# Copies of raw weights and squares in PSUM, in two quarters of a feed-forward layer

## The chip, the cores and the metric

The kernel runs on one core of one Trainium2 chip. The metric is the device time of one execution in microseconds; the median of several executions is compared. Before the change it is 1726.33 us (three executions, 1724.89 to 1726.98).

## The reference

One layer of a streaming encoder for 1024 prompt rows and 32 sample rows, 1024 wide: two attention mixers, a gated merge, and a feed-forward part of width 4096. The change lies in the feed-forward part:

```python
h = x + jnp.einsum('bld,de->ble', m, w_out)
u = jnp.einsum('bld,df->blf', rmsnorm(h, g_ffn), w_up)
return h + jnp.einsum('blf,fd->bld', jnp.square(jax.nn.relu(u)), w_down)
```

All of it is in fp32.

## The kernel before

**Products.** An fp32 product is made of three matmuls on operands of the type FP32R: each operand is split into a high part, which ScalarE makes by a cast copy, and a low part, the operand less its high part, which VectorE or GpSimd makes by a subtraction. `three` (one 128-row step) issues wh·xh, wh·xl and wl·xh into one PSUM bank. Weights come in blocks of 128x512 (`raw`, a load on SyncE's queue), `pair` makes the two parts of a block, `parts` those of an activation.

**The feed-forward part.** The rows are worked in groups; the first big group of 512 columns (x is held transposed) goes through `ffn_group`, in four quarters of 1024 hidden units. Quarters 0 and 1 multiply plainly, quarters 2 and 3 in `deep_quarters`. There, each quarter has a step of `ups` for j = 0 to 3 (two blocks of 24 matmuls 128x512 each: u = relu(x·W_up)², in halves of 256 columns) and then `down` for i = 0 to 3. `down` doesn't multiply the four weight blocks w11, w12, w21, w22 of W_down with the four quarters of the activations in eight products, but takes seven (Strassen's way in Winograd's form), of 12 matmuls 128x256 each. For that it needs four sums of weight blocks (s1 = w21 + w22, w21 + w11, w11 + s1, w12 + that) and four sums of activations (T1 to T4), and `gather` adds the products into y. `done` in `ups` makes the activations' parts: in the first block of a step (i = 0) U11 and T1; in the second (i = 1) U21 and U22 (`both`), T3, T2 and T4. The first product of `down` uses U11, the second U21.

**Sums for the second group.** The same weight sums are also written to DRAM (`self.sums`), for w_up too, since a later group reads them there. For w_up the four additions are made by `sums` after a step, and the four stores follow.

**Who sets the order.** Every instruction is recorded by `Plan.record` and issued later by `Plan.run`, engine by engine, in the order of a list scheduler: it takes the ready instruction of the lowest rank (FAST, PREP, MAIN, FILL, SLOW), by times of its own cost model (`cost`), in which VectorE's operations with two inputs in SBUF and GpSimd's lock each other out (`locks`). All instructions have line 412, where `issue` calls them (413 after the change). So an edit in `deep_quarters` can move instructions of the whole stretch. On the chip, each engine works through its queue in that order, and an instruction that waits holds those behind it.

**PSUM.** A core has eight banks of 128x512 fp32: here six with the name `pj` and two with `pd`. In `deep_quarters` `bank()` hands them out in a turn of six pj and two pd. GpSimd can't take part in anything in PSUM in this kernel: whatever it subtracts or adds lies in SBUF.

**Names in the profile.** `ru` are the tiles of relu and square, `xh`/`xl` parts of the last block of activations (`sets`, `third`, `more` hold the sums' parts), `wh`/`wl` parts of weights, `raw`, `wst`, `rb` raw weights, `y` the output sums, `gh`/`gl` the parts of the second group's attention outputs; `xl<-rb`, `xl<-raw` and `xl<-wst` are weight parts kept in the room of x's low part.

Of the kernel before, what the change touches and what calls it, by code (L numbers as in the profile page):

```python
# [47 lines left out]
DEEP = 2  # L48
RAWS, PAIRS, WIDE = 8, 7, 2
ORDER = (*range(8, 16), 5, 6, 7)  # L50
WAIT = (1000, 0, 1500, 0)
# [369 lines left out]
class Layer:  # L421
# [1265 lines left out]
    def ffn_group(self, g, late):  # L1687
# [79 lines left out]
        self.ahead = [row("w_up", 4 * DEEP, i) for i in range(2)]  # L1767
        self.ahead_raws, self.ahead_sums = raws, sums

    def deep_quarters(self, g, qs):  # L1770

        nc, a = self.nc, self.a
        raws, sums = self.ahead_raws, self.ahead_sums
        V, G, add, sub = nc.vector, nc.gpsimd, nc.vector.tensor_add, nc.vector.tensor_sub
# [16 lines left out]
        g.acc = [g.ss[:, cs] for cs in g.chunks]  # L1791
        banks = [lambda: self.bank("pj")[:, :n]] * 6 + [lambda: self.bank("pd")[:, :n]] * 2
        bank = lambda: self.turn("bank", banks)

# [16 lines left out]

        def pair(st, eng):

            with nc.rank(PREP):
                h, l = self.turn("weights", pairs[wide[0]])
                nc.scalar.copy(h, st)
                eng.tensor_sub(l, st, h.bitcast(F32))
            return h, l

        def parts(place, z, eng):  # L1820
            nc.scalar.copy(place[0], z)
            eng.tensor_sub(place[1], z, place[0].bitcast(F32))

        def ups(j, i, units, r0=None):
# [3 lines left out]
            def done(c, cs, ps):  # L1828
                nc.scalar.activation(r, ps, AF.Relu)
                nc.scalar.activation(r, r, AF.Square)  # L1830
                lo, hi = r[:, :n], r[:, n:]
                if i == 0:
                    parts(U11[j], lo, V)
                    sub(lo, lo, hi)
                    parts(T1[j], lo, G)
                    return
                parts(both[j], r, V)
                t, u12 = r0[:, :n], r0[:, n:]
# [9 lines left out]

        def weights(t, engs):

            with nc.rank(PREP):
                w11, w12, w21, w22 = (raw(a["w_down"][i, t]) for i in range(4))
                s1 = raw()

            def keep(i, z):
                with nc.rank(PREP):
                    nc.sync.dma_start(self.sums["w_down", t][i], z)

            def total(out, x, y):
                with nc.rank(PREP):  # L1860
                    add(out, x, y)

            engs = iter(engs)
            yield pair(w11, next(engs))
            yield pair(w12, next(engs))
            total(s1, w21, w22)
            keep(0, s1)
            yield pair(s1, next(engs))
            total(w21, w11, w21)
            keep(2, w21)  # L1870
            total(w11, w11, s1)
            keep(1, w11)
            yield pair(w11, next(engs))
            total(w12, w12, w11)
            keep(3, w12)
            yield pair(w12, next(engs))
            yield pair(w21, next(engs))
            yield pair(w22, next(engs))

# [10 lines left out]
        def down(q, i):  # L1890

            wt = weights(4 * q + i, (V, G, G, G, G, G, G) if q == 3 else (V, G, V, G, G, V, G))

# [33 lines left out]
        for q in qs:  # L1927
            for j in range(4):
                r, st = None, []
                for i in range(2):  # L1930
                    if self.ahead:
                        new, units = self.ahead.pop(0)
                    else:
                        with nc.rank(PREP):
                            new = [raw(a["w_up"][2 * i + k, 4 * q + j]) for k in range(2)]
                        units = [pair(z, G) for z in new]
                    st += new
                    r = ups(j, i, units, r)
                sums("w_up", 4 * q + j, *st)
            if q == 3:  # L1940
# [90 lines left out]
```

## Time and profile before

| what | us |
| --- | --- |
| median of three executions | 1726.33 |
| the profiled execution | 1727.03 |
| its span in the trace | 1725.2 |
| PE busy | 1700.6 |
| VectorE busy | 1273.5 |
| ScalarE busy | 1081.6 |
| GpSimd busy | 1027.0 |
| the stretch of quarters 2 and 3 in the span | 1107 to 1294 |
| PE busy in that stretch | 181.24 of 187 |
| VectorE, ScalarE, GpSimd busy in it | 166.91, 97.57, 148.76 |

About 1.8 us lie outside the span. Times in the views are from the start of the span. In the views a row of a timeline gives start, duration, engine, operation, out<-in, shape and count, and in brackets the time that the engine had been idle and what ended it. The ends of matmuls are modelled, so that consecutive ones overlap, and the distance of their starts is their pace.

### The profile page before, as it was taken

The page shows a single profiled execution, that of the slowest core. Times are in us where ns is not written, and L with a number is a line of the kernel's source. Part 1 is how long each engine was busy: PE and PEld are TensorE (multiplying, and loading weights), DVE is VectorE, ACT ScalarE, POOL GpSimd, SP SyncE. Part 2 cuts the span into 40 slices and gives each one's busy share as a digit, 9 for nine tenths or more (in the row PEclk, how much of TensorE's full clock was granted, in tenths as well). Part 3 has the DMA queues.
Part 4 walks back from the last instruction along what each step waited for, and adds up shares of the span by engine and source line. Part 5 has one row for each costly group of instructions (what it writes and reads, how often), then busy time and mean ns, then how long its engine had stood idle before and what let it go on. Part 6 is the DMA issues. An engine that isn't in the chain of part 4 may idle for free. (4 is left out here: it accounts for less than half of the span.)

```text
span 1725.2 us, 33597 instructions
## 1 busy us (share of the span) xinstructions
PE 1700.6 (99%) x11442; PEld 1577.4 (91%) x11442; DVE 1273.5 (74%) x2599; ACT 1081.6 (63%) x2352; POOL 1027.0 (60%) x850
## 2 busy tenths in 40 slices
PE   8999999999999999999999999999999999999999
PEld 7989999999999989988888888888899999999998
DVE  8567778999556645898986677699975684666577
ACT  6556798873255777777666575554645675747473
POOL 5342333344366675798874454569788794646563
PEclk9999999999999999999999999999999999999999
DMA  7353452444566678556375565546676656555664
GB/s 222 112 168 89 138 170 87 144 142 135 169 183 169 177 205 232 169 153 190 127 234 186 171 199 172 199 173 228 215 258 194 184 168 196 177 173 171 177 185 170
DMA packets 195962, 302.41 MB, mean 175 GB/s; under 512 B 36048, under 2 KB 67376, under 8 KB 195792
## 3 DMA queue, kind: packets, MB, share of 16 engines
q1 hardware_dynamic: 195360, 299.94, 57.0%
q8 instruction: 90, 1.47, 0.4%
q14 instruction: 80, 0.66, 0.1%
q10 hardware_dynamic: 432, 0.34, 0.1%
HBM read 212.39 MB, written 87.70 MB: 174 GB/s over the span
## 5 line engine op out<-in xcount | busy, mean ns | idle before, releaser
L412 PE MATMUL pj<-xh,wh 128*128 128x272 f32 (+2 forms) x1771 | 592.9, 336 | 3.6 <-ACT xh L412 2.9
L412 PE MATMUL pj<-xl,wh 128*128 128x272 f32 (+2 forms) x1771 | 593.9, 336 | 1.2 <-DVE xl L412 1.2
L412 PE MATMUL pj<-xh,wl 128*128 128x272 f32 (+2 forms) x1771 | 593.8, 336 | 0.0
L412 POOL TENSOR_TENSOR wl<-wst,wh 128x512 fp32r<-128x512 f32 x234 | 329.1, 1413 | 206.6 <-ACT wh L412 199.8
L412 PEld LDWEIGHTS pj<-xh,wh 128*128 128x128 f32 x1771 | 333.3, 188 | 33.2 <-ACT xh L412 3.3
L412 PEld LDWEIGHTS pj<-xl,wh 128*128 128x128 f32 x1771 | 333.8, 189 | 29.4 <-DVE xl L412 1.7
L412 PEld LDWEIGHTS pj<-xh,wl 128*128 128x128 f32 x1771 | 333.4, 189 | 27.8
L412 ACT CAST wh<-wst 128x512 fp32r<-128x512 f32 x254 | 156.3, 619 | 108.4 <-PE pj L412 69.5
L412 POOL TENSOR_TENSOR wl<-raw,wh 128x512 fp32r<-128x512 f32 x103 | 157.3, 1535 | 82.8 <-ACT wh L412 65.2
L412 ACT CAST wh<-raw 128x512 fp32r<-128x512 f32 x147 | 90.5, 622 | 81.0 <-PE pj L412 43.2
L412 POOL TENSOR_TENSOR p<-p,rem 128x895 f32<-128x895 f32 (+6 forms) x66 | 106.1, 1621 | 30.5 <-DVE rem L412 26.0
L412 DVE TENSOR_TENSOR tt<-t,tt 128x512 fp32r<-128x512 f32 (+2 forms) x168 | 99.4, 619 | 28.4 <-ACT tt L412 27.4
L412 DVE TENSOR_TENSOR_SCAN rem<-rem 128x896 f32<-128x896 f32 (+6 forms) x66 | 114.9, 1762 | 6.1 <-ACT rem L412 5.8
L412 ACT ACTIVATE junk<-score,cand 128x384 bf16<-128x384 f32 (+1 forms) x124 | 116.0, 936 | 4.3 <-DVE cand L412 2.3
L412 ACT CAST tt<-t 128x512 fp32r<-128x512 f32 (+2 forms) x168 | 84.7, 540 | 45.2 <-PE t L412 33.7
L412 PEld LDWEIGHTS o<-tt,v 128*128 128x128 f32 x640 | 92.6, 188 | 13.2 <-DVE tt L412 2.6
L412 PE MATMUL o<-tt,v 128*128 128x256 f32 (+1 forms) x640 | 99.1, 277 | 3.6 <-DVE tt L412 2.0
L412 PE MATMUL pj<-gh,wh 128*128 128x272 f32 x352 | 101.2, 289 | 0.0
L412 PE MATMUL pj<-gh,wl 128*128 128x272 f32 x352 | 101.1, 289 | 0.0
L412 PE MATMUL pj<-gl,wh 128*128 128x272 f32 x352 | 101.1, 288 | 0.0
L412 PE MATMUL s<-k,q 128*128 128x384 f32 (+5 forms) x384 | 94.0, 354 | 1.4 <-DMA q<-dq 0.8
L412 POOL TENSOR_TENSOR wl<-rb,wh 128x512 fp32r<-128x512 f32 x49 | 70.7, 1443 | 40.6 <-ACT wh L412 34.5
(411 smaller groups left out, 4239.4 us busy)
## 6 DMA issues: line engine op xcount, KB each, us to landing
q<-dq SPq DMA_DIRECT2D x64, 256.0 KB, 5.4
raw<-w_up SPq DMA_DIRECT2D x52, 256.0 KB, 3.2
raw<-w_down SPq DMA_DIRECT2D x52, 256.0 KB, 3.1
k<-dk SPq DMA_DIRECT2D x48, 256.0 KB, 4.0
v<-dv SPq DMA_DIRECT2D x48, 256.0 KB, 4.2
wst<-w_g SPq DMA_DIRECT2D x42, 256.0 KB, 3.4
wst<-w_up SPq DMA_DIRECT2D x37, 256.0 KB, 2.9
wst<-w_down SPq DMA_DIRECT2D x36, 256.0 KB, 3.5
```

Of the source, the lines that this page charges most:

```text
L412: fn(*args, **kw)
```

## The change

In `deep_quarters` alone:

- `copy(z)`: ScalarE copies a raw weight block from SBUF to a `pd` bank. For w_up this is w11 of a step (seven of eight; the first step's blocks are loaded ahead in `ffn_group`), for w_down w11 and w22, 16 copies.
- The low part of a copied block is now made by VectorE, from the copy in PSUM; the low parts of all other blocks by GpSimd. Before, all of w_up were GpSimd's, and of w_down's seven three VectorE's in quarter 2 (one in quarter 3).
- `add_up` makes the four sums, with a copied block read from PSUM where there is one, and each sum's store right behind it; for w_down all four sums stand together after the third pair, and w22's pair is made ahead of them, though used last. Before, the sums stood between the pairs.
- The squares go to the PSUM bank that the block's matmuls filled, and the parts and sums of the activations are read there. For i = 0 the square is now two instructions of 256 columns, since the second half stays in SBUF.
- `bank()` gives the six pj banks in turn; the pd banks are for the copies.

The number of matmuls is the same. The diff:

```diff
--- before.py
+++ after.py
@@ -47,6 +47,7 @@
 SUMS = 3
 DEEP = 2
 RAWS, PAIRS, WIDE = 8, 7, 2
+COPIES = ((0,), (0, 2))
 ORDER = (*range(8, 16), 5, 6, 7)
 WAIT = (1000, 0, 1500, 0)
 TOPK = (("a", [2, 3, 4, 7], (2, 7), 0), ("b", [5, 6, 8], (5, 6), 16))
@@ -1765,12 +1766,12 @@
                             (self.scales if q else self.squares)(g)
                     sums(name, 4 * q + j, *raw)
         self.ahead = [row("w_up", 4 * DEEP, i) for i in range(2)]
-        self.ahead_raws, self.ahead_sums = raws, sums
+        self.ahead_raws = raws
 
     def deep_quarters(self, g, qs):
 
         nc, a = self.nc, self.a
-        raws, sums = self.ahead_raws, self.ahead_sums
+        raws = self.ahead_raws
         V, G, add, sub = nc.vector, nc.gpsimd, nc.vector.tensor_add, nc.vector.tensor_sub
         n = 256
         flat = [z.rearrange("p k t -> p (k t)") for z in (g.mh, g.ml)]
@@ -1789,8 +1790,13 @@
         both = [[z[:, (4 + 2 * k) * n:(6 + 2 * k) * n] for z in flat] for k in range(4)]
         g.chunks = [slice(0, n), slice(n, 2 * n)]
         g.acc = [g.ss[:, cs] for cs in g.chunks]
-        banks = [lambda: self.bank("pj")[:, :n]] * 6 + [lambda: self.bank("pd")[:, :n]] * 2
-        bank = lambda: self.turn("bank", banks)
+        bank = lambda: self.bank("pj")[:, :n]
+
+        def copy(z):
+
+            ps = self.bank("pd")
+            nc.scalar.copy(ps, z)
+            return ps
 
         tmp = nc.open("tmp", "right")
         raws = [raws + [lambda: nc.tile(g.pool, [128, W1], F32, "raw", tag="pb", bufs=3)] * 3,
@@ -1809,12 +1815,15 @@
                 nc.sync.dma_start(z, src)
             return z
 
-        def pair(st, eng):
+        def pair(st, ps=None):
 
             with nc.rank(PREP):
                 h, l = self.turn("weights", pairs[wide[0]])
                 nc.scalar.copy(h, st)
-                eng.tensor_sub(l, st, h.bitcast(F32))
+                if ps is None:
+                    G.tensor_sub(l, st, h.bitcast(F32))
+                else:
+                    sub(l, ps, h.bitcast(F32))
             return h, l
 
         def parts(place, z, eng):
@@ -1827,14 +1836,17 @@
 
             def done(c, cs, ps):
                 nc.scalar.activation(r, ps, AF.Relu)
-                nc.scalar.activation(r, r, AF.Square)
-                lo, hi = r[:, :n], r[:, n:]
                 if i == 0:
+                    lo, t, u12 = ps[:, :n], r[:, :n], r[:, n:]
+                    nc.scalar.activation(lo, t, AF.Square)
+                    nc.scalar.activation(u12, u12, AF.Square)
                     parts(U11[j], lo, V)
-                    sub(lo, lo, hi)
-                    parts(T1[j], lo, G)
+                    sub(t, lo, u12)
+                    parts(T1[j], t, G)
                     return
-                parts(both[j], r, V)
+                nc.scalar.activation(ps, r, AF.Square)
+                lo, hi = ps[:, :n], ps[:, n:]
+                parts(both[j], ps, V)
                 t, u12 = r0[:, :n], r0[:, n:]
                 sub(u12, hi, u12)
                 parts(T3[j], u12, G)
@@ -1846,36 +1858,31 @@
             self.column_block(units, lambda k, cs: (g.h[:, k, cs], g.l[:, k, cs]), done, [slice(0, W1)])
             return r
 
-        def weights(t, engs):
+        def add_up(name, t, w11, w12, w21, w22, s1=None, p11=None, p12=None, p22=None):
+
+            s1 = w22 if s1 is None else s1
+            f = lambda x, y: y if x is None else x
+            for i, out, x, y in ((0, s1, f(p22, w22), w21), (2, w21, f(p11, w11), w21), (1, w11, f(p11, w11), s1),
+                                 (3, w12, f(p12, w12), w11)):
+                add(out, x, y)
+                nc.sync.dma_start(self.sums[name, t][i], out)
+
+        def weights(t):
 
             with nc.rank(PREP):
                 w11, w12, w21, w22 = (raw(a["w_down"][i, t]) for i in range(4))
                 s1 = raw()
-
-            def keep(i, z):
-                with nc.rank(PREP):
-                    nc.sync.dma_start(self.sums["w_down", t][i], z)
-
-            def total(out, x, y):
-                with nc.rank(PREP):
-                    add(out, x, y)
-
-            engs = iter(engs)
-            yield pair(w11, next(engs))
-            yield pair(w12, next(engs))
-            total(s1, w21, w22)
-            keep(0, s1)
-            yield pair(s1, next(engs))
-            total(w21, w11, w21)
-            keep(2, w21)
-            total(w11, w11, s1)
-            keep(1, w11)
-            yield pair(w11, next(engs))
-            total(w12, w12, w11)
-            keep(3, w12)
-            yield pair(w12, next(engs))
-            yield pair(w21, next(engs))
-            yield pair(w22, next(engs))
+                p11, p12, p22 = (copy(z) if i in COPIES[1] else None for i, z in enumerate((w11, w12, w22)))
+            yield pair(w11, p11)
+            yield pair(w12, p12)
+            x22 = pair(w22, p22)
+            with nc.rank(PREP):
+                add_up("w_down", t, w11, w12, w21, w22, s1, p11, p12, p22)
+            yield pair(s1)
+            yield pair(w11)
+            yield pair(w12)
+            yield pair(w21)
+            yield x22
 
         def product(wt, xs, ps=None):
             first = ps is None
@@ -1889,7 +1896,7 @@
 
         def down(q, i):
 
-            wt = weights(4 * q + i, (V, G, G, G, G, G, G) if q == 3 else (V, G, V, G, G, V, G))
+            wt = weights(4 * q + i)
 
             def gather(e, c, ps, sign, when):
                 cs = g.chunks[c]
@@ -1926,17 +1933,22 @@
 
         for q in qs:
             for j in range(4):
-                r, st = None, []
+                r, st, ps = None, [], {}
                 for i in range(2):
                     if self.ahead:
                         new, units = self.ahead.pop(0)
                     else:
                         with nc.rank(PREP):
                             new = [raw(a["w_up"][2 * i + k, 4 * q + j]) for k in range(2)]
-                        units = [pair(z, G) for z in new]
+                            if i == 0 and 0 in COPIES[0]:
+                                ps["p11"] = copy(new[0])
+                            if i and 2 in COPIES[0]:
+                                ps["p22"] = copy(new[1])
+                        got = [ps.get("p11"), None] if i == 0 else [None, ps.get("p22")]
+                        units = [pair(z, p) for z, p in zip(new, got)]
                     st += new
                     r = ups(j, i, units, r)
-                sums("w_up", 4 * q + j, *st)
+                add_up("w_up", 4 * q + j, *st, **ps)
             if q == 3:
                 self.reload(g, 2)
             for i in range(4):
```

How the queues change, at the end of quarter 3's up blocks. ScalarE before; the last block's relu and square are the two rows ACTIVATE ru_14467, U21 and U22 get their high parts by CAST xh1_222<-ru_14467 128x512, and wh are high parts of weights:

```order
L412 CAST xl0_221<-rb_224 128x512 [waits DMAHW5_49,PE_49]
L412 CAST wh_14501<-raw_14494 128x512 [waits DVE_49]
L412 ACTIVATE ru_14467<-pj_14468 128x512 [waits PE_49,Activation_49]
L412 ACTIVATE ru_14467<-ru_14467 128x512 [waits Activation_49]
L412 CAST wh_14504<-raw_14490 128x512 [waits DVE_49]
L412 CAST xh1_222<-ru_14467 128x512 [waits Activation_49]
L412 CAST wh_14506<-raw_14491 128x512 [waits DVE_49]
```

ScalarE after at the same place (the last block's square now goes to its bank, pj_14483):

```order
L413 CAST wh_14525<-raw_14507 128x512 [waits PE_49]
L413 ACTIVATE ru_14482<-pj_14483 128x512 [waits PE_49,Pool_49]
L413 ACTIVATE pj_14483<-ru_14482 128x512 [waits Activation_49]
L413 CAST wh_14527<-raw_14508 128x512 [waits PE_49]
L413 CAST xh1_222<-pj_14483 128x512 [waits DVE_49]
L413 CAST sets_14265<-ru_14474 128x256
L413 CAST sets_14265<-ru_14474 128x256 [waits DVE_49]
L413 CAST xh1_222<-pj_14483 128x256 [waits DVE_49]
```

In both a weight cast stands between the square and the cast of U21 and U22: before it waits for a sum of VectorE's, now for PE, which frees its room. The cast of U21 and U22 now waits for VectorE, which reads the same bank ahead of it.

VectorE before, at the same place; the four rows raw are the weight sums of a w_down step, and ru_14459<-ru_14467,ru_14459 is the first difference of the last block (u12):

```order
L412 TENSOR_TENSOR ru_14459<-ru_14459 128x256 [waits DVE_49]
L412 TENSOR_TENSOR raw_14494<-raw_14492,raw_14493 128x512 [waits DMAHW4_49,DMAHW3_49,DMAHW1_49]
L412 TENSOR_TENSOR raw_14492<-raw_14490,raw_14492 128x512 [waits DVE_49]
L412 TENSOR_TENSOR raw_14490<-raw_14490,raw_14494 128x512 [waits DMAHW2_49,DVE_49]
L412 TENSOR_TENSOR raw_14491<-raw_14491,raw_14490 128x512 [waits DMAHW0_49,DVE_49,Pool_49]
L412 TENSOR_TENSOR ru_14459<-ru_14467,ru_14459 128x256 [waits Activation_49]
L412 TENSOR_TENSOR xl1_223<-ru_14467,xh1_222 128x512 [waits Activation_49]
L412 SCALAR_TENSOR_TENSOR ru_14459<-ru_14459,ru_14467 128x256 [waits Pool_49]
L412 TENSOR_TENSOR y0_6599<-pj_14474,y0_6599 128x256 [waits PE_49]
L412 SCALAR_TENSOR_TENSOR ru_14467<-ru_14459,ru_14467 128x256 [waits DVE_49]
```

VectorE after:

```order
L413 TENSOR_TENSOR ru_14474<-pj_14475,ru_14474 128x256 [waits Activation_49]
L413 TENSOR_TENSOR xl1_223<-pj_14475,xh1_222 128x256
L413 TENSOR_TENSOR xl0_221<-pd_14535,xl0_221 128x512 [waits PE_49,Activation_49]
L413 TENSOR_TENSOR y0_6599<-pj_14491,y0_6599 128x256 [waits PE_49]
L413 TENSOR_TENSOR ru_14474<-pj_14483,ru_14474 128x256 [waits DVE_49,Activation_49]
L413 SCALAR_TENSOR_TENSOR ru_14474<-ru_14474,pj_14483 128x256 [waits Activation_49,Pool_49]
L413 TENSOR_TENSOR xl1_223<-pj_14483,xh1_222 128x512
L413 SCALAR_TENSOR_TENSOR pj_14483<-ru_14474,pj_14483 128x256 [waits DVE_49]
L413 TENSOR_TENSOR sets_14265<-ru_14474,sets_14265 128x256 [waits Activation_49]
```

The four sums no longer stand ahead of the difference; the y row, a gather, does, and an operation on the bank pj_14483 waits for ScalarE's casts of it.

ScalarE before, at the end of quarter 2's up blocks (the last block's rows are ru_14319):

```order
L412 CAST third_14267<-ru_14303 128x256 [waits DVE_49]
L412 CAST xh1_222<-ru_14311 128x256 [waits DVE_49]
L412 ACTIVATE ru_14319<-pj_14320 128x512 [waits PE_49,Activation_49,Pool_49]
L412 ACTIVATE ru_14319<-ru_14319 128x512 [waits Activation_49]
L412 CAST xh1_222<-ru_14319 128x512 [waits Activation_49]
```

ScalarE after there; the two COPY rows are the copies of w11 and w22 of the first w_down step:

```order
L413 COPY pd_14375<-raw_14370 128x512 [waits DMAHW5_49,DVE_49]
L413 CAST xh1_222<-ru_14314 128x256 [waits DVE_49]
L413 COPY pd_14376<-raw_14373 128x512 [waits DMAHW0_49,DVE_49]
L413 CAST wh_14364<-raw_14348 128x512 [waits PE_49]
L413 ACTIVATE ru_14322<-pj_14323 128x512 [waits PE_49]
L413 ACTIVATE pj_14323<-ru_14322 128x512 [waits Activation_49]
L413 CAST wh_14366<-rb_224 128x512 [waits DVE_49,PE_49]
L413 CAST xh1_222<-pj_14323 128x512 [waits DVE_49]
```

The copies, which wait for a load each (DMAHW) and for VectorE, stand ahead of the last block's relu, and one weight cast too; the cast of the bank pj_14323 waits for VectorE.

## The prediction

> **What bounds the kernel now.** I read the page's first part, then the table of windows over the last two quarters of the first group, then PE's waits there, and then the timelines of ScalarE (ACT), VectorE (DVE) and GpSimd (POOL) ahead of the two largest waits.
>
> ```profile
> PE 1700.6 (99%) x11442; PEld 1577.4 (91%) x11442; DVE 1273.5 (74%) x2599; ACT 1081.6 (63%) x2352; POOL 1027.0 (60%) x850
> ```
>
> TensorE bounds the program: it is busy in 1700.6 of 1725.2 us. The change leaves the number of matmuls as it is, so it can only win back time in which PE stands still or runs below its pace, and only in the stretch that it touches. The table of windows shows that stretch (us; busy time and instructions of PE, PEld, DVE, ACT, POOL; granted clock; DMA share; GB/s):
>
> ```profile
> 1150.00:1162.00 12.00, 9.78 (x77) 9.13 (x76) 10.85 (x21) 4.97 (x10) 4.82 (x4) 1.00 0.66 224
> 1162.00:1182.00 20.00, 19.95 (x167) 19.62 (x166) 19.82 (x30) 9.25 (x16) 14.56 (x10) 1.00 0.73 250
> 1182.00:1200.00 18.00, 16.93 (x118) 15.26 (x119) 14.15 (x18) 7.48 (x13) 17.35 (x12) 1.00 0.60 191
> 1242.00:1252.00 10.00, 7.89 (x53) 7.39 (x52) 9.88 (x11) 6.33 (x13) 10.00 (x8) 0.83 1.05 407
> 1262.00:1282.00 20.00, 20.00 (x170) 20.00 (x169) 16.63 (x37) 11.51 (x19) 16.59 (x13) 1.00 0.87 282
> 1282.00:1294.00 12.00, 11.69 (x92) 11.25 (x92) 5.40 (x13) 5.43 (x9) 11.56 (x9) 1.00 0.90 290
> ```
>
> 1262 to 1282 is a clean stretch of w_down products: 20.00 / 170 = 0.1176 us for one 128x256 matmul. By that pace the 77 matmuls of 1150 to 1162 need 9.06 us, so 2.94 are lost there; the 53 of 1242 to 1252 need 6.23, so 3.77 are lost. In the other two windows wider matmuls are mixed in, so I take only what isn't busy: 1.07 (18.00 - 16.93) and 0.31 (12.00 - 11.69). With 0.05 from 1162 to 1182 the stage loses **8.1 us**. Since a modelled end hides part of each gap, the true loss may be some 1 us more; I carry 9.2 as the ceiling. PE's waits (engine, what it waited for: us in total, times, longest), first for 1149 to 1200, then for 1240 to 1294, name who is late:
>
> ```profile
> PE pj L412 <- DVE xl L412: 1.2, 1, 1.2
> PE pj L412 <- ACT xh L412: 0.8, 1, 0.8
> PE pd L412 <- DVE y L412: 0.8, 1, 0.8
> PE pd L412 <- POOL wl L412: 0.3, 1, 0.3
> PE pj L412 <- DVE y L412: 0.2, 1, 0.2
> ```
>
> ```profile
> PE pj L412 <- ACT xh L412: 2.1, 1, 2.1
> PE pj L412 <- DVE pj L412: 0.3, 1, 0.3
> ```
>
> Both large losses stand where a quarter's up blocks end and its w_down products begin: PE needs the parts of the last block's activations, and these are late. The timelines around the second such boundary show why, PE first, then ACT, then DVE (start, us, operation, in brackets the idle time before it and what ended it):
>
> ```profile
> 1239.65 0.40 PE L412 MATMUL pj<-xh,wl 128*128 128x512 f32 x1
> ...
> 1243.15 0.28 PE L412 MATMUL pd<-xl,wh 128*128 128x256 f32 x1
> 1245.49 0.38 PE L412 MATMUL pj<-xh,wh 128*128 128x256 f32 x1 [2.06 <-ACT xh L412]
> ...
> 1247.15 0.41 PE L412 MATMUL pj<-xl,wh 128*128 128x256 f32 x1
> ```
>
> ```profile
> 1241.11 0.62 ACT L412 CAST xl<-rb 128x512 fp32r<-128x512 f32 x1
> 1241.63 0.62 ACT L412 CAST wh<-raw 128x512 fp32r<-128x512 f32 x1
> 1242.15 0.59 ACT L412 ACTIVATE ru<-pj 128x512 f32<-128x512 f32 x1
> 1242.77 0.63 ACT L412 ACTIVATE ru<-ru 128x512 f32<-128x512 f32 x1
> 1244.30 0.62 ACT L412 CAST wh<-raw 128x512 fp32r<-128x512 f32 x1 [0.90 <-DVE raw L412]
> 1244.82 0.61 ACT L412 CAST xh<-ru 128x512 fp32r<-128x512 f32 x1
> ```
>
> ```profile
> 1240.68 5.25 DVE L412 TENSOR_TENSOR raw<-raw 128x512 f32<-128x512 f32 x4
> 1245.86 1.51 DVE L412 TENSOR_TENSOR ru<-ru 128x256 f32<-128x256 f32 x1
> ```
>
> The last up matmul starts at 1239.65, and PE has other products until 1243.3. But the square is done only at 1243.4, and the cast xh<-ru that PE waits for stands on ACT behind a weight cast that waits for DVE's sums. Those four sums take 5.25 us, 1.3 each. After the wait of 2.06 us PE falls to the pitch of half a clock (0.41 in place of 0.28 for one modelled matmul); this is the 0.83 in the windows' clock column, and makes the other 1.7 us of the 3.77.
>
> At the first boundary the chain is of the same kind (POOL, DVE, ACT and PE):
>
> ```profile
> 1138.09 5.78 POOL L412 TENSOR_TENSOR wl<-raw,wh 128x512 fp32r<-128x512 f32 x1 [3.11 <-issue]
> ```
>
> ```profile
> 1144.60 1.50 DVE L412 SCALAR_TENSOR_TENSOR ru<-ru 128x256 f32<-128x256 f32 x1 [1.91 <-POOL xl L412]
> ```
>
> ```profile
> 1151.76 0.41 ACT L412 CAST xh<-ru 128x256 fp32r<-128x256 f32 x1 [2.08 <-DVE ru L412]
> 1152.07 0.59 ACT L412 ACTIVATE ru<-pj 128x512 f32<-128x512 f32 x1
> ```
>
> ```profile
> 1149.93 0.39 PE L412 MATMUL pj<-xh,wl 128*128 128x512 f32 x1
> ...
> 1154.03 0.50 PE L412 MATMUL pj<-xh,wh 128*128 128x256 f32 x2 [0.83 <-ACT xh L412]
> ```
>
> DVE and POOL hold each other up: POOL's subtraction took 5.78 us, DVE then waited for POOL, and the relu of the last block began at 1152.07, 1.7 us after that block's last matmul had ended (1149.93 + 0.39). PE would have gone on at 1153.2 (1154.03 less its 0.83). How far the two stretch each other, the groups of this stage say (count: minimum/median/maximum ns):
>
> ```profile
> L412 DVE TENSOR_TENSOR y<-pj,y x23: 405/412/692, 1100.3 to 1279.9; 128x256 f32<-128x256 f32 x21, 128x512 f32<-128x512 f32 x2
> L412 DVE TENSOR_TENSOR raw<-raw x32: 677/1220/1821, 1133.2 to 1271.6; 128x512 f32<-128x512 f32 x32
> L412 DVE TENSOR_TENSOR wl<-raw,wh x10: 677/1286/1796, 1138.0 to 1232.5; 128x512 fp32r<-128x512 f32 x10
> ```
>
> ```profile
> L412 POOL TENSOR_TENSOR wl<-raw,wh x43: 1297/1711/5775, 1106.1 to 1264.5; 128x512 fp32r<-128x512 f32 x43
> ```
>
> An operation of DVE with an input in PSUM never took over 0.69 us. One with both inputs in SBUF takes between 0.68 and 1.8, and POOL's go up to 5.8.
>
> **The change, part by part.** *Copies.* ScalarE makes 7 copies of w_up blocks and 16 of w_down blocks, 128x512 each. No ScalarE write to PSUM stands in this trace; the nearest rows are
>
> ```profile
> L412 ACT CAST wh<-raw 128x512 fp32r<-128x512 f32 x53 | 32.0, 619 | 30.5 <-DVE raw L412 14.1 <-PE pj L412 10.4 <-PE pd L412 3.1
> L412 ACT ACTIVATE ru<-ru 128x512 f32<-128x512 f32 x16 | 10.1, 632 | 0.3
> ```
>
> so 23 x 0.619 to 0.632 = 14.2 to 14.5 us more on ACT, plus a second square in 8 blocks. I take the lower end, the cast, which reads the same weight blocks. ACT has room: the windows give it 4.97 of 12, 9.25 of 20 and 11.51 of 20 busy. This work costs nothing by its sum, but each copy is a place in ACT's queue at which the relu behind it may have to wait (third rival).
>
> *Sums and low parts.* DVE's weight subtractions rise from 16 (three in each w_down step of the third quarter, one in each of the fourth) to 23 (two in each, and the copied w_up blocks), but all of them now read PSUM: 23 x 0.69 = 15.9 us in place of 16 x 1.29 = 20.6. POOL loses the seven of w_up, 7 x 1.71 = 12.0 us. Of the four sums of a w_down step three now read PSUM, of a w_up step two: 0.69 in place of 1.22. So the 5.25 us of four sums would be 3 x 0.69 + 1.22 = 3.3, and they no longer stand all together between the square and its parts: the order puts DVE's difference and the cast directly behind the square. Bounds for this on PE's time: nothing (if the sums were never the last thing waited for) and the whole 8.1.
>
> *Squares in PSUM.* The cast xh and DVE's subtraction now read one bank. The order shows waits of one on the other there: the cast of the last block waits for DVE's difference, and DVE's next operation on that bank waits for the cast. The chain at the second boundary, from these rows: last up matmul done at 1240.1, relu free to start by 1240.3, +0.6 relu, +0.63 square = 1241.5, behind a gather of 0.41 DVE's difference 0.41 = 1242.4, the cast 0.62 = 1243.0. PE needs it at 1243.3. So the wait of 2.06 goes with 0.3 us to spare, and DVE's low part follows by 0.41 + 0.69 at 1244.1, just ahead of its use. Were these operands left in SBUF, the difference could be put beside the cast and the chain would be 0.4 shorter: this is what the squares in PSUM cost, at nothing while the 0.3 us hold.
>
> The Trainium skill, "PSUM — Partial Sum Buffer", section "PSUM bank collisions raise a hardware error", says that ScalarE and VectorE may not touch one bank at the same time, reading included, so that their accesses must be ordered by waits. That rule speaks against this part of the change: it is the mechanism of the first rival below, whose price would then be the right one.
>
> *What is left of each loss.* Second boundary: of 3.77 I leave 0.3 (the margin is as thin), as the half clock goes with the wait: -3.5. First boundary: of 2.94 I leave 0.4: -2.5. 1182 to 1200: its 0.8 (a bank freed late by DVE) gets better with a shorter DVE queue, but the turn of banks shrinks from eight to six; of 1.07 I leave 0.6: -0.5. 1282 to 1294: 0.31 before; two low parts there stand behind casts and subtractions for the next group, so 0 to +0.8; I take 0. **Sum: -6.5 us**, bounds -9.2 and 0.
>
> The half clock is the one price which could go otherwise. The Trainium skill, "TensorE: Matmul & The Clock Gate", section "What's actually happening", lets the clock fall only after a free-running idle window of about 3.4 us; the wait here was 2.06 us and the clock fell all the same. By that rule the dip would not be owed to this wait and could stay, and the gain would be 1.7 less, 4.8 us.
>
> The profiled run took 1727.03 us for a span of 1725.2, 0.7 above the median of 1726.33. I take the gain from the median: 1726.33 - 6.5 = **1719.8 us**.
>
> **The rivals.** *First: the shared bank gives half of it back.* If DVE's difference stands behind one more SBUF operation of the stretched kind (1.29 in place of a gather's 0.41), the cast is 0.9 late at each boundary, which eats the 0.3 and stalls PE 0.6 twice; the wait may again bring the half clock at one of them (1.7), and low parts are late by as much (0.4). 1.2 + 1.7 + 0.4 = 3.3 less: 1723.1. For it: DVE was busy 19.82 of 20 us in 1162 to 1182. Against: its queue gets shorter.
>
> *Second: nothing moves by more than can be measured.* The late step might be another than I think, say the number of ACT's casts ahead of the relu (at the second boundary two stood between 1241.1 and 1242.15). The waits then move to other places and the sum stays: 1725 to 1728.
>
> *Third, slower: a copy that waits for its load holds up the relu.* In the new order of ACT two copies of w_down blocks stand ahead of the last block's relu, square and cast. A copy waits for the load of its block, and SyncE's loads stand behind stores of sums:
>
> ```profile
> 1155.91 1.14 SPq L412 DMA_DIRECT2D raw<-w_down  x2
> ```
>
> ```profile
> raw<-w_down SPq DMA_DIRECT2D x52, 256.0 KB, 3.1
> ```
>
> If the load is issued as late as the one in this row (the last of its step before), it lands at about 1159; the relu follows at 1159.6, and with 0.6 + 0.63 + 0.41 + 0.62 the cast ends at 1161.9, where PE needs it at 1153.2: 8.7 lost in place of 2.94, +5.8. At both boundaries: +5.8 and 8.7 - 3.77 = +4.9, 1737.0. At one of them alone, with the gain of the other: about 1728. It decides from the point at which a copy's block lands later than some 3 us before the boundary's relu. Against it: now each sum's store is issued right behind its sum, and the sums are done earlier, so I expect the load some 5 us ahead of its use.
>
> **How the numbers follow.** The first theory, that most of the loss goes, has 0.62: 1717.1 (all of 9.2) to 1722.9. The first rival 0.16 (1722.5 to 1724.5), the second 0.10 (1725 to 1728), the third 0.12 (1728 to 1737, mostly above 1729.8). The range of 1717.0 to 1727.5 leaves out the third and a part of the second. A measurement of this kernel can tell about 0.2% from no change: 3.45 us, so faster is below 1722.9 and slower above 1729.8. Faster 0.62 + 0.03 of the first rival = 0.65; same 0.13 + 0.10 + 0.02 = 0.25; slower 0.10.
>
> **What would show it.** In the new profile PE's wait <- ACT xh of 2.06 should be under 0.5, and the window behind that boundary should have a granted clock of 1.00. The first boundary's two waits (1.2 and 0.8 here) should come to under 0.6. DVE's sums and weight subtractions with an input pd should be at 0.68 to 0.70 without a stretched one, and POOL's maximum of 5.78 should be gone. ACT's copies should be at 0.6 us and wait for no DMA. It would be wrong if a copy on ACT shows idle time that a raw<-w_down load ended, with a PE wait of several us behind it, or if the dip of the clock turns up without a wait.

## The result, and the profile after

After the change the median is 1716.09 us (six executions, 1713.8 to 1718.03) against 1726.50 (six, 1724.89 to 1727.97): a ratio of 0.9941, with a 95% interval of 0.9928 to 0.9953, or 10.4 us. The forecast was 1719.8, with a range of 1717.0 to 1727.5. The sign and the places were right; the gain was larger than forecast, and the time lies 0.9 us below the range.

The windows of the kernel after, at the same times as before, with the whole stretch first (its profiled execution took 1716.12 us for a span of 1714.3). The second boundary now comes earlier, at 1233 to 1237, so the window from 1242 no longer holds it:

```profile
1107.00:1294.00 187.00, 186.93 (x1211) 170.49 (x1210) 128.30 (x249) 112.94 (x223) 122.96 (x103) 1.00 0.71 240
1150.00:1162.00 12.00, 12.00 (x104) 12.00 (x103) 7.09 (x17) 6.31 (x13) 6.95 (x6) 1.00 0.57 195
1162.00:1182.00 20.00, 20.00 (x172) 20.00 (x171) 12.39 (x24) 10.46 (x20) 17.04 (x14) 1.00 0.61 186
1182.00:1200.00 18.00, 18.00 (x108) 15.87 (x107) 13.74 (x24) 9.06 (x18) 11.98 (x10) 1.00 0.74 249
1242.00:1252.00 10.00, 10.00 (x87) 10.00 (x85) 9.96 (x22) 3.35 (x7) 6.18 (x6) 1.00 0.50 182
1282.00:1294.00 12.00, 12.00 (x98) 12.00 (x97) 4.23 (x9) 6.47 (x11) 6.42 (x5) 1.00 0.82 278
```

PE is busy in 186.93 of 187 us. The view of waits lists not a single wait of PE from 1107 to 1294, both boundaries included, and the granted clock is 1.00 throughout. In the same 187 us PE gets through 1211 matmuls instead of 1127. VectorE's busy time falls from 166.91 to 128.30 us, GpSimd's from 148.76 to 122.96, and ScalarE's grows from 97.57 to 112.94.

The chain at the second boundary, ScalarE and then PE (the block's last wide matmul, and the pair that needs the cast xh):

```profile
1233.74 0.60 ACT L413 ACTIVATE ru<-pj 128x512 f32<-128x512 f32 x1
1234.36 0.60 ACT L413 ACTIVATE pj<-ru 128x512 f32<-128x512 f32 x1
1234.90 0.60 ACT L413 CAST wh<-raw 128x512 fp32r<-128x512 f32 x1
1235.64 0.59 ACT L413 CAST xh<-pj 128x512 fp32r<-128x512 f32 x1
```

```profile
1233.01 0.40 PE L413 MATMUL pj<-xh,wl 128*128 128x512 f32 x1
...
1236.75 0.40 PE L413 MATMUL pj<-xh,wh 128*128 128x256 f32 x2
```

From the end of the last wide matmul (1233.41) to the end of the cast (1236.23) it is 2.8 us, and PE asks for it 0.5 us later. The forecast worked out 2.9 and 0.3.

VectorE's activation operations, before and then after (count: minimum/median/maximum ns, over both shapes), are the rows that the forecast did not look at:

```profile
L412 DVE TENSOR_TENSOR xl<-ru,xh x18: 409/1201/1775, 1114.3 to 1253.1; 128x256 fp32r<-128x256 f32 x10, 128x512 fp32r<-128x512 f32 x8
L412 DVE TENSOR_TENSOR ru<-ru x16: 410/414/1515, 1115.6 to 1245.9; 128x256 f32<-128x256 f32 x16
L412 DVE SCALAR_TENSOR_TENSOR ru<-ru x16: 410/784/1514, 1123.0 to 1250.2; 128x256 f32<-128x256 f32 x16
```

```profile
L413 DVE TENSOR_TENSOR xl<-pj,xh x18: 406/420/685, 1113.5 to 1239.4; 128x256 fp32r<-128x256 f32 x10, 128x512 fp32r<-128x512 f32 x8
L413 DVE TENSOR_TENSOR ru<-pj,ru x16: 407/424/426, 1113.1 to 1235.2; 128x256 f32<-128x256 f32 x16
L413 DVE SCALAR_TENSOR_TENSOR ru<-ru,pj x8: 410/416/422, 1119.4 to 1236.3; 128x256 f32<-128x256 f32 x8
L413 DVE SCALAR_TENSOR_TENSOR pj<-ru,pj x8: 414/428/430, 1121.4 to 1237.4; 128x256 f32<-128x256 f32 x8
```

With one operand in PSUM none of these 50 takes longer than the shortest of its shape by more than a few hundredths of a us. With both in SBUF some took 1.5 to 1.8. GpSimd's rows of before, with a median of 1.71 us and a maximum of 5.78, have become

```profile
L413 POOL TENSOR_TENSOR wl<-raw,wh x37: 1283/1297/1757, 1108.4 to 1267.1; 128x512 fp32r<-128x512 f32 x37
```

### The profile page after: what moved, and what is told of

Same layout as the page of the kernel before. It is cut to its first block, busy times and chain, and to the rows that moved or that the text cites. A ratio compares the mean times of both kernels' runs of the same rounds, so it can differ in the third digit from the quotient of the medians.

```text
span 1714.3 us, 33657 instructions
## 1 busy us (share of the span) xinstructions
PE 1696.1 (99%) x11442; PEld 1575.9 (92%) x11442; DVE 1227.0 (72%) x2606; ACT 1091.5 (64%) x2383; POOL 1000.8 (58%) x843
## 4 chain that ended last, share of the span: by engine, by line
PE 91%; DVE 4%; DMA 3%; issue 1%; ACT 1%; POOL 0%; SPq 0%; ACTq 0%; POOLq 0%; DVEq 0%
PE pj L413 65%; PE s L413 15%; PE t L413 5%; PE o L413 4%; PE pd L413 3%; DMA k<-dk 1%; DVE xl L413 1%; DMA do<-o 0%; DVE pj L413 0%; DMA o<-do 0%; DMA q<-dq 0%; DVE y L413 0%; DVE rem L413 0%; SPq L413 0%; DMA ist<-w_ia 0%
## 5 line engine op out<-in xcount | busy, mean ns | idle before, releaser
L413 PE MATMUL pj<-xh,wl 128*128 128x272 f32 (+2 forms) x1795 | 599.8, 335 | 0.0
L413 PEld LDWEIGHTS pj<-xh,wh 128*128 128x128 f32 x1795 | 337.2, 188 | 30.4 <-DVE y L413 1.3
L413 PEld LDWEIGHTS pj<-xl,wh 128*128 128x128 f32 x1795 | 337.8, 188 | 27.8
L413 PEld LDWEIGHTS pj<-xh,wl 128*128 128x128 f32 x1795 | 337.3, 188 | 27.7
L413 POOL TENSOR_TENSOR wl<-raw,wh 128x512 fp32r<-128x512 f32 x98 | 136.1, 1393 | 89.6 <-ACT wh L413 74.1
```

The source lines that it names most:

```text
L413: fn(*args, **kw)
```

## The experiments

The theories at the start: one, that VectorE's reading of PSUM ends the mutual stretching with GpSimd and that this is the gain; two, that the gain is the new order of sums and pairs; three, that it is the squares in PSUM. A fourth came out of the first four runs. "Waits" below is the sum of PE's waits from 1107 to 1294, and "VectorE busy" is its time in these 187 us. Before has 5.7 and 166.9, after 0 and 128.3. Gains are against the median of before in the same round, 1725.3 to 1725.9. One thing holds for all of these runs: the planner makes the queues anew for each edit, so an edit changes what the chip does and where the instructions stand.

**Operands back to SBUF, one part at a time.** First no copies, everything else as after:

```diff
-            ps = self.bank("pd")
-            nc.scalar.copy(ps, z)
-            return ps
+            return z
```

> The kernel after, but no block is copied: what read the copy in PSUM reads the raw block in SBUF, on the same engine and at the same place in the program. Theory one (what is won comes from VectorE reading one operand in PSUM, so that VectorE and GpSimd no longer stretch each other): the waits at the two boundaries come back, with stretched rows of 1.2 to 1.8 us on VectorE, 1722 to 1726 us. Theory two (it comes from the order of sums and pairs and from which engine makes which low part): 1715 to 1718, no PE wait over 0.5 us. Theory three (it comes from the squares in PSUM): 1715 to 1718 as well.

Measured: 1719.45 us, ratio 0.9958 (0.9945 to 0.9972). Waits 2.7, VectorE busy 151.9. This lies between the expectations: without any copy 6.5 us of the gain are still there.

Then the copies without the squares:

```diff
-                nc.scalar.activation(ps, r, AF.Square)
-                lo, hi = ps[:, :n], ps[:, n:]
+                nc.scalar.activation(r, r, AF.Square)
+                lo, hi = r[:, :n], r[:, n:]
```

(and i = 0 in the same way.)

> The kernel after with the squares written back to SBUF as before, the copies kept. Theories one and two: 1715 to 1718, since the boundary's chain gets shorter by the wait of one engine on the other, though four subtractions in each step now have both operands in SBUF. Theory three: 1722 to 1726, with the wait on the cast xh at the second boundary back.

Measured: 1719.17, ratio 0.9961 (0.9948 to 0.9973). Waits 1.8, VectorE busy 142.7. A gain of 6.7, again between the two.

Then both edits together, so that only the order is left:

> The kernel after with neither copies nor squares in PSUM: only the new order of sums and pairs, the new share of low parts between VectorE and GpSimd, and the banks in a turn of six are left. Theory one: 1723 to 1727, most of the loss of before. Theory two: 1715 to 1718. Theory three: 1723 to 1727.

Measured: 1727.44, ratio 1.0004 (0.9995 to 1.0013). Waits 7.1, VectorE busy 164.3. Theory two has fallen: the new program order alone wins nothing. Its trace also shows how the loss comes about at the second boundary, VectorE and then ScalarE:

```profile
1238.69 1.78 DVE L413 TENSOR_TENSOR wst<-wst 128x512 f32<-128x512 f32 x1
1240.39 1.50 DVE L413 TENSOR_TENSOR ru<-ru 128x256 f32<-128x256 f32 x1
```

```profile
1241.92 0.41 ACT L413 CAST xh<-ru 128x256 fp32r<-128x256 f32 x1 [1.90 <-DVE ru L413]
1242.23 0.63 ACT L413 ACTIVATE ru<-ru 128x512 f32<-128x512 f32 x1
```

A sum of 1.78 us and a difference of 1.50 us (0.68 and 0.41 where nothing stretches them) keep ScalarE waiting for 1.90 us, and the last block's square stands behind that wait.

And the squares alone, put into the kernel before:

> The kernel before with the squares written to PSUM as after, and nothing else of the change. Theory one: 1724 to 1727, as the sums of raw blocks are still stretched ahead of the boundary. Theory two: 1724 to 1727. Theory three: 1716 to 1719.

Measured: 1717.75, ratio 0.9952 (0.9940 to 0.9965). Waits 1.5, VectorE busy 147.8. This is in the range of theory three. Theory one as I had put it expected 1724 to 1727, because the sums of raw blocks would still be stretched. They are as stretched as before, and the time is 8.2 us better all the same. The rows of this run for the sums on VectorE and the subtractions on GpSimd:

```profile
L412 DVE TENSOR_TENSOR raw<-raw x32: 678/1219/1784, 1124.0 to 1253.5; 128x512 f32<-128x512 f32 x32
```

```profile
L412 POOL TENSOR_TENSOR wl<-raw,wh x42: 1284/1575/1766, 1105.7 to 1249.4; 128x512 fp32r<-128x512 f32 x42
```

But the sums no longer stand where they did: the planner has put none of them into the 6 us ahead of the second boundary's difference (ru<-pj,ru), and VectorE even stands idle there:

```profile
1233.22 1.24 DVE L412 TENSOR_TENSOR xl<-raw,xl 128x512 fp32r<-128x512 f32 x1 [1.11 <-ACT xl L412]
1235.98 0.43 DVE L412 TENSOR_TENSOR y<-pj,y 128x256 f32<-128x256 f32 x1 [1.53 <-PE pj L412]
1236.33 0.41 DVE L412 TENSOR_TENSOR ru<-pj,ru 128x256 f32<-128x256 f32 x1
```

So most of the gain comes without shorter sums. Whether the sums did harm at the boundary, where the forecast had put them, this run doesn't say.

Copies and squares stand in for one another: with one of them 6.5 to 8.2 us are won, with both 10. It doesn't go by the number of operations that are taken off two SBUF operands (some 60 with the copies, 50 with the squares). That either part wins most of the gain can mean two things: VectorE's queue gets shorter, or the two engines stop holding each other up.

**A longer queue without sharing, and with it.** 46 subtractions were added to the kernel after, first with the copy in PSUM as an operand, then with the raw block in SBUF:

```diff
-                    sub(l, ps, h.bitcast(F32))
+                    for _ in range(3):
+                        sub(l, ps, h.bitcast(F32))
```

> The kernel after, with each of the 23 subtractions that read a copy in PSUM made three times: 46 more VectorE operations of 0.68 us, 31 us, all with one operand in PSUM. VectorE's busy time in the stage (1107 to 1294) goes from 128 to about 160 us, near the 164 and 167 of the new order alone and of before. Theory one as it now stands (what decides is how long VectorE's queue is, whatever makes it long): the waits come back, 1722 to 1727 us. Theory four (what decides is that VectorE and GpSimd stretch each other's operations, and plain work of VectorE does no harm): 1715 to 1718.

Measured: 1715.39, ratio 0.9943 (0.9931 to 0.9956). No wait of PE, VectorE busy 151.6.

```diff
+                    for _ in range(2):
+                        sub(l, st, h.bitcast(F32))
                     sub(l, ps, h.bitcast(F32))
```

> The same number of added subtractions, but the 46 read the raw block in SBUF, so that they share with GpSimd. VectorE's busy time in the stage: 160 us and more, as a part of them is stretched to 1.2 to 1.8 us, and GpSimd's subtractions are stretched too (median above 1.4 us). Theory one: 1723 to 1730, by the length of VectorE's queue. Theory four: 1722 to 1728, and well above the run with the same number of added operations in PSUM.

Measured: 1723.88, ratio 0.9990 (0.9981 to 0.9999), with executions from 1721.12 to 1726.94; the trace is of the longest. Waits 4.9, VectorE busy 169.4. The added rows, in PSUM and then in SBUF:

```profile
L413 DVE TENSOR_TENSOR wl<-pd,wh x60: 676/682/692, 1109.1 to 1243.9; 128x512 fp32r<-128x512 f32 x60
```

```profile
L413 DVE TENSOR_TENSOR wl<-raw,wh x32: 677/1182/1784, 1112.6 to 1254.5; 128x512 fp32r<-128x512 f32 x32
```

Against the kernel after, the same work costs nothing in PSUM and 8 us in SBUF. At 151.6 us of VectorE's time nothing is lost, while the run without copies loses at 151.9. So the length of the queue alone does not decide, as far as 151.6 us go (the 160 that I expected and the 166.9 of before were not reached). Theory four is left, but this pair does not prove it: the planner counts the sharing and has moved other instructions as well. Counted from start to start of the matmuls, the run with the added operations in SBUF loses nothing at either boundary, 3.5 us between about 1165 and 1200, where PE waits for two low parts of GpSimd's at 1.7 us each in place of 1.3, and 4.8 us in the last w_down steps. The last is a place where the order alone can lose as much, as the last pair of runs shows. The Trainium skill, "SBUF — State Buffer", section "Who interferes with whom", says that VectorE contends with a GpSimd instruction that reads SBUF when both its inputs lie in SBUF, and not with one input there. These two traces agree (0.68 us at most 0.69, against 0.68 to 1.78).

**Which copies, and ScalarE's room.** Without the seven copies of w_up (`COPIES = ((), (0, 2))`):

> The kernel after without the seven copies of w_up; their low parts go back to GpSimd. Both theories: 1716 to 1719, since the boundary's queue holds the sums of w_down; the last boundary's wait at most 0.5 us.

Measured: 1717.19, ratio 0.9951 (0.9938 to 0.9963), no wait of PE. The copies of w_up are worth no more than these runs can tell. Every copy made twice:

> The kernel after with every copy to PSUM made twice: 23 more ScalarE operations of 0.59 us, 13.6 us, at the places in its queue at which a relu may stand behind. If ScalarE's queue has the room that its busy share of 60% says: 1715 to 1718. If the copies stand in the way of relu, square and cast (the third rival of the forecast, in small): a wait <- ACT xh or sets of 0.5 to 1.5 us at the boundaries, 1718 to 1720.

Measured: 1714.85, ratio 0.9939 (0.9925 to 0.9952), no wait of PE, ScalarE busy 123.2 of 187. ScalarE has the room, and the third rival has no ground here.

**Chip or planner.** The planner also believes in the sharing, so a new place of an operand changes the order as well. Two kernels try to part the two: one has its operands in SBUF but tells the planner that the operations which read PSUM in the kernel after do not share; the other is the kernel after with the planner told that they do. Neither repeats the order of its partner exactly; the sequence of PE's products differs too.

```diff
     def locks(self, op, out, ins, args):
+        if self.told:
+            return False
```

> The new order alone (no copies, squares in SBUF), but the planner is told that the operations which read PSUM in the kernel after do so here too, so that it doesn't count them as sharing with GpSimd: the order comes near that of after, while on the chip all operands lie in SBUF. If what decides happens on the chip (VectorE and GpSimd stretch each other): 1723 to 1729, with waits of PE of 7 us and more in the stage. If what decides is the order that the planner finds once it believes the operations free: 1715 to 1719.

Measured: 1736.21, ratio 1.0055 (1.0043 to 1.0068), slower than either expectation. Waits 13.6, the largest 3.6 at the first boundary. It is 8.8 us slower than the same operands with an honest planner (1727.44). Against the kernel after, from start to start, it loses 12.8 us at the first boundary and 4.6 at the second.

```diff
-        if any(x.tensor.name in self.banks for x in ins):
+        if any(x.tensor.name in self.banks for x in ins) and not self.told:
```

> The converse: the kernel after, but in these two quarters the planner counts VectorE's operations with an operand in PSUM as sharing with GpSimd. The order is one for a chip that stretches them, the chip doesn't. If what decides happens on the chip: 1715 to 1718, PE waits under 0.5 us. If the order decides: 1720 to 1726.

Measured: 1725.67, ratio 0.9998 (0.9989 to 1.0007). This is in the range for an order that decides (1720 to 1726): the whole gain is gone, though VectorE's rows with an operand in PSUM are as short as after (`raw<-pd,raw` at 0.68, VectorE busy 122.1). But it is lost in another place. There is no wait of PE at either boundary; all four stand between 1265 and 1275, in the last w_down steps, which lose 9.4 us against the kernel after:

```profile
1266.06 0.50 PE L414 MATMUL pj<-more,wh 128*128 128x256 f32 x2 [1.10 <-DVE pj L414]
1270.60 0.39 PE L414 MATMUL pj<-xh,xl 128*128 128x256 f32 x1 [2.86 <-ACT xl L414]
1271.64 0.80 PE L414 MATMUL pj<-sets,wh 128*128 128x256 f32 x2 [0.54 <-ACT wh L414]
1274.73 0.80 PE L414 MATMUL pj<-xh,xl 128*128 128x256 f32 x2 [2.29 <-POOL xl L414]
```

ScalarE's queue there:

```profile
1266.99 2.03 ACT L414 CAST gh<-o 128x544 fp32r<-128x544 f32 x3 [2.68 <-DMA o<-do]
1269.38 0.65 ACT L414 CAST gh<-o 128x544 fp32r<-128x544 f32 x1 [0.36 <-DMA o<-do]
1269.93 0.61 ACT L414 CAST xl<-raw 128x512 fp32r<-128x512 f32 x1
```

The weight cast that PE waits for (xl<-raw) stands behind four casts for the next group, and these wait for a load of o. GpSimd's queue shows the same for its low part:

```profile
1267.71 5.74 POOL L414 TENSOR_TENSOR gl<-o,gh 128x544 fp32r<-128x544 f32 x4 [3.58 <-DMA o<-do]
1273.40 1.27 POOL L414 TENSOR_TENSOR xl<-raw,xl 128x512 fp32r<-128x512 f32 x1
```

In the kernel after, the last weight cast into that room stands ahead of all casts gh on ScalarE:

```profile
1256.58 0.62 ACT L413 CAST xl<-raw 128x512 fp32r<-128x512 f32 x1 [4.02 <-PE pj L413]
...
1259.96 1.19 ACT L413 CAST gh<-o 128x544 fp32r<-128x544 f32 x2
```

So with the operands in PSUM nothing is lost at the boundaries, whatever the planner was told; with all of them in SBUF both orders lose there. The order decides whether as much is lost elsewhere. Both parts of the two expectations were too simple, and how much of the 10 us is the chip's sharing and how much is the order that the planner can now choose, these runs do not part.

**The half clock.** To get a wait of known length, the last block's relu was repeated in the kernel after:

```diff
-                nc.scalar.activation(r, ps, AF.Relu)
+                for _ in range(1 + (late[0] if i and j == 3 else 0)):
+                    nc.scalar.activation(r, ps, AF.Relu)
```

> The kernel after, with the relu of the last up block made five more times (0.5 us each) in both quarters, so that the boundary's chain ends 2.6 us later. The chain had about 0.5 us to spare at the second boundary, so PE should wait some 2 us at each. If the half clock of before was owed to a wait of that length, the granted clock falls behind one wait or both, and each fall costs some 1.7 us: 1720 + 1.7 to 1720 + 3.4. If it wasn't, the clock stays at 1.00 and the time is near 1720.

> The same with eight more relus at the first boundary (4.2 us later, a wait of some 3.7 us) and two at the second (1.0 us later, a wait of 0.5). If the fall of the clock comes with the length of the wait: a fall at the first, none at the second; 1716 + 3.7 + 0.5 + 1.7 = 1722. If it comes with a free-running window alone, it may fall behind neither: 1720.

Measured: 1716.14 (two executions, 1716.04 and 1716.24) and 1714.54 (1713.73 and 1715.34). The first shows two waits of 0.2 us, the second none: the planner knew of the later relu and put other products ahead, so the runs say nothing on the clock. They do say that a chain some 4 us longer at the first boundary costs nothing where the planner knows its length. The clock has to be read from the waits that other runs happened to have. Windows behind one in before (2.06 us, ended at 1245.5), in the run with 46 more subtractions in SBUF (2.09 us, ended at 1275.1), and in the new order alone (1.52 us, ended at 1180.6):

```profile
1246.00:1251.00 5.00, 4.95 (x29) 4.65 (x29) 5.00 (x5) 3.38 (x7) 5.00 (x4) 0.66 1.05 408
```

```profile
1276.00:1280.00 4.00, 4.00 (x26) 4.00 (x25) 0.63 (x2) 1.97 (x5) 4.00 (x5) 0.66 0.74 272
```

```profile
1178.00:1182.00 4.00, 2.48 (x22) 2.27 (x20) 4.00 (x6) 1.45 (x3) 4.00 (x3) 1.00 0.65 219
1182.00:1186.00 4.00, 3.71 (x32) 3.50 (x31) 3.10 (x5) 2.60 (x5) 4.00 (x4) 1.00 0.73 177
```

In this stage a wait of 2.06 us or more had a stretch at half clock behind it, and one of up to 1.52 us had none. But the length of one wait is not the whole of it. Far ahead of this stage, near 26 us, the run with 46 more subtractions in SBUF and the second run with added relus have a half clock as well (0.50 from 26.8 to 30.2 us in the latter), behind waits of at most 1.25 us; before has the same wait there (1.26 us) and no half clock. How much PE was busy in the 3.4 us ahead sorts the places somewhat better (1.31 to 1.78 us ahead of these four falls, 1.88 ahead of the end of the wait of 1.52 us), but not cleanly: in before 1.70 us brought no fall near 26. This was seen, not made: what sets the bound stays open.

## Why the prediction was right and wrong

**What bounds it.** Right. PE's waits at the two boundaries, and the smaller ones between and behind them, were the loss, and the change removes them all. That the stretching of VectorE and GpSimd has a part in it is borne out: stretched rows stand in the chain of the run with the new order alone, runs with all these operands in SBUF lose at the boundaries under either order, and 46 added operations cost nothing where they don't share. That it is the whole cause is not shown, since the planner's order always changed with it.

**Size of the loss.** This is the step that failed for the time: "the stage loses **8.1 us**", with 9.2 as the ceiling. Followed from start to start, the 7051st to the 8061st matmul take 160.3 us in the trace of before and 150.1 in that of after, so 10.1 us were lost and won. By the same count the terms of before are 3.1 at the first boundary (I had 2.94), 0.3 from 1162 to 1182 (0.05), 2.1 from 1182 to 1200 (1.07), 4.0 at the second boundary (3.77) and 0.9 from 1282 to 1294 (0.31), less 0.3 that after still shows near 1252. The term most off is 1182 to 1200: I took only what isn't busy there because wide matmuls were mixed in, and a modelled end covers a part of every wait. Each of the seven recorded waits cost 0.2 to 0.3 us more than its row says. I had seen this, but allowed 1 us for it and then made the smaller count the base of the sum. Even the ceiling, from which the lower bound of the range came, was 0.9 us too low.

**What is left of each loss.** Wrong by 1.6 us: I left 0.3, 0.4 and 0.6 at three places and the whole 0.3 from 1282 on, and nothing is left at any of them. With the 2.0 us of size this makes up the difference between the gain of 6.5 that I forecast and the 10.1 in the trace.

**Copies.** The cost of nothing on ScalarE was right (0.59 us each where I took 0.62, and even twice as many cost nothing). The sign that no copy waits for a DMA was missed once: the first copy of w_up waited 1.5 us for its load, and no wait of PE followed. That the sums no longer stand ahead of the difference came true in the kernel after. The new program order alone did not bring it about: with all operands in SBUF the planner still put a stretched sum ahead of the second boundary, and the time is 1727.44.

**Squares in PSUM.** Here the mechanism failed: "this is what the squares in PSUM cost, at nothing while the 0.3 us hold". I put the whole gain on the copies, the sums and the order, and looked at the squares only as a cost, the wait of one engine on the other for the shared bank, with nothing on the other side. Alone they win 8.2 us, and the copies without them 6.7. They take 50 operations of the stretch, those of the boundaries' chains among them, off two SBUF operands, and I had not looked up the rows of those operations in the trace of before, where xl<-ru,xh has a median of 1.20 us. How much of the 8.2 us is shorter operations and how much the order that the planner makes with them stays open. The wait for the shared bank is there, on VectorE:

```profile
1236.33 0.42 DVE L413 SCALAR_TENSOR_TENSOR ru<-ru,pj 128x256 f32<-128x256 f32 x1 [0.72 <-ACT xh L413]
```

PE waited for none of it, and the chain up to the cast took 2.8 us where I had 2.9. The Trainium skill, "PSUM — Partial Sum Buffer", section "PSUM bank collisions raise a hardware error", has ScalarE and VectorE kept off one bank at the same time; the order does this here, and PE's time does not show its price.

**The half clock.** Borne out: with the wait gone there was none, and in this stage none came without a wait. No run made a wait of a chosen length. The Trainium skill's clock rule ("TensorE: Matmul & The Clock Gate", section "What's actually happening") asks for an idle window of 3.4 us; here waits of 2.06 and 2.09 were enough. The measurement decides, and the rival price of 1.7 us did not come. The stretch itself was as long as that window: (1 - 0.66) x 2 x 5 us = 3.4 in before, if the clock fell to the 0.50 that the other trace shows.

**The rivals.** The shared bank (first) cost PE nothing, and no copy held up a relu so that PE waited (third). The second, that the waits only move, is what happens in the kernel whose planner was told wrongly; the wait there was for weights behind another group's casts.

## What to carry to other kernels

Look at every row of VectorE with two SBUF operands, not only at the one that PE waits for: if its median is far above its minimum while GpSimd is busy, one operand in PSUM may be worth a copy by an engine with room. Where the order is planned from a model of the chip, the model has to know of the change, or the gain is lost at another place. And for the room that is to be won, count the instructions that get through in a window at the clean pace, and not the recorded waits.

## What the runs showed of the hardware

VectorE's 128x512 operations on two SBUF operands take 0.68 to 1.8 us beside GpSimd's work, and GpSimd's 1.27 to 1.83 us (5.8 once in before, 4.3 once in the run planned as if in PSUM, 3.7 once in the run with the new order alone); with one operand in PSUM VectorE's stay at 0.67 to 0.70. ScalarE's copy of a 128x512 block to PSUM takes 0.59 us, against 0.62 for the cast of such a block to SBUF. In this stage a wait of PE of 2.06 us or more had a stretch of 3.4 us (once 6.8, behind two waits) at half clock behind it, and one of up to 1.52 us had none; ahead of the stage one of 1.25 us had one in two traces.
